# First quarter of the feed-forward input product as eight plain products instead of seven half-block products

## The chip, the core and the metric

The kernel runs on one core of one Trainium2 chip. The metric is device time in microseconds (us) of one execution; the median of several runs is compared. Engines: PE (TensorE, matrix products; PEld is its weight load), DVE (VectorE), ACT (ScalarE), POOL (GpSimd) and SP (SyncE, here a queue that issues transfers). Each engine takes its instructions in the order of its own queue and waits on semaphores for the others.

## The reference, cut to what matters

One block of an encoder: three token mixers, their gated sum through an output projection onto the residual x, then an RMS norm and a feed-forward part with squared ReLU. Sizes: 512 tokens, 1024 channels, 4096 hidden channels, all float32.

```python
        x = x + mixed @ w_out[l]

        u = _rmsnorm(x, g_mlp[l]) @ w_ff1[l]
        x = x + jnp.square(jax.nn.relu(u)) @ w_ff2[l]
```

## The kernel before

Every large product is made of three products in float32r: an operand is split into hi (rounded to float32r by ACT) and lo (what is left, by DVE), and hi*hi + hi*lo + lo*hi are added in PSUM. A weight tile is 128 x 1024 (512 KB); SP loads it as float32, ACT writes hi (`whi`), DVE writes lo (`wlo`), each into a ring of four buffers.

Since the norm's factor is one number per token, it is left out of u and put in behind: relu and square commute with it up to r squared, and `onto` (line 1137) multiplies by `r2` or `nr2` from `norm1` (line 1129).

The feed-forward part has four quarters of 1024 hidden channels (loop at line 1147). Each is `ff1` (line 1052: u times a quarter of w_ff1, then relu and square into `R`) and then ff2 (R times a quarter of w_ff2, added onto x). Both use Strassen's scheme in Winograd's form: a product of 2 x 2 blocks as seven half-block products instead of eight. For that sums of blocks of the weights are needed (loads that add onto what lies in the buffer, `w_more`, issued by POOL, line 186) and sums of blocks of the left operand. In ff1 a half-block product is 48 products of 256 columns (`product_f`, line 1032); in ff2 it is 24 products of 512 columns (`product`, line 162).

The left operand of ff1 is u, x transposed: `u_tile(f)` (line 936) makes four PE transposes of one block of 128 channels into one of two PSUM banks (tag `tr`) and ACT copies it out, times the gain of the norm, into `U`. `u_pair` splits a block of U, `u_form` a sum of blocks of U. The seven forms `us[0]` to `us[6]` are made once, during quarter one, and used by all four quarters. In `out_proj` (line 972), the last thing before, four u_tiles stand after the halves of the last product (line 1020), and the loads of the first quarter's weights are issued by `f_first` (line 965) into rings of tiles: `rq` (four buffers) and `raw` (three buffers).

Order: a scheduler puts the instructions of each engine in order when the kernel is built, near the order of the code but not bound to it, and gives a tile the buffer of one that is done; so a transfer waits on its queue until the buffer's last reader is done. SP's queue is strictly in order: a load that waits for its buffer holds up those behind it.

## Time and profile before

| what | value |
|---|---|
| median of 3 runs | 1144.14 us (1142.69 to 1144.30) |
| profiled execution | 1144.42 us |
| its span | 1142.6 us |
| PE busy | 1121.3 us (98%), 5784 instructions |
| DVE busy | 840.0 us (74%) |
| ACT busy | 701.4 us (61%) |
| mean granted clock of PE | 0.993 |

The profile is of one execution. The span runs from the first instruction to the last; the execution's time is 1.8 us longer. Busy time of PE counts overlapping products once, and each product's end is modelled, so a product's cost is read from the distance of starts in a stage without waits. "PEclk" or "granted clock" is the share of full speed that the chip grants PE: 1.0 is 2.4 GHz, and the lower level is 1.2 GHz; a value between is a mean over a stretch.

### The profile page before, as it was taken

What the parts mean: (1) busy time and instruction counts of PE and PEld (TensorE: products, weight loads), DVE (VectorE), ACT (ScalarE), POOL (GpSimd) and SP (SyncE); (2) the same over time, 40 slices, a digit from 0 to 9 for tenths busy, and PEclk for the clock granted to TensorE, in tenths of its full rate; (3) what the DMA queues carried; (4) which work ended last, traced back from release to release, by engine and by line L of the source; (5) the groups of instructions that cost most, each with busy time, mean ns of one, the idle gap of its engine ahead of it and who ended that gap; (6) DMA issues with size and microseconds to landing.
All of it is one profiled execution on the core that took longest, in us unless ns stands there. A gap on an engine that the chain in (4) does not pass through costs nothing.

```text
span 1142.6 us, 15585 instructions
## 1 busy us (share of the span) xinstructions
PE 1121.3 (98%) x5784; PEld 954.2 (84%) x5784; DVE 840.0 (74%) x1266; ACT 701.4 (61%) x1169; POOL 99.7 (9%) x159
## 2 busy tenths in 40 slices
PE   9899999999999999999999999999989999999998
PEld 6678888888888888878877888888888898998997
DVE  5998777764337877564488788679688779688788
ACT  7855468556426767754378788535667466475573
POOL 0012201000001000000000000001101111101110
PEclk9999999999999999999999999999989999999999
DMA  9969715114332221262222221748848978878774
GB/s 359 360 144 260 223 57 183 57 43 135 110 100 74 93 74 52 74 203 92 92 100 95 98 79 62 217 130 197 193 104 206 221 185 189 217 198 209 176 191 112
DMA packets 54275, 170.32 MB, mean 149 GB/s; under 512 B 5684, under 2 KB 12212, under 8 KB 54200
## 3 DMA queue, kind: packets, MB, share of 16 engines
q1 hardware_dynamic: 41192, 123.12, 30.8%
q0 software_dynamic: 12864, 46.14, 21.1%
q8 instruction: 45, 0.74, 0.3%
q14 instruction: 30, 0.25, 0.1%
q10 hardware_dynamic: 144, 0.07, 0.0%
HBM read 160.91 MB, written 8.40 MB: 148 GB/s over the span
## 4 chain that ended last, share of the span: by engine, by line
PE 53%; DVE 3%; ACT 3%; DMA 2%; issue 1%; DVEq 0%; ACTq 0%; POOLq 0%
PE pj L85 7%; PE pj L86 7%; PE pj L87 7%; PE q L171 3%; PE q L170 3%; PE q L172 3%; PE q L1044 3%; PE q L1045 3%; PE q L1043 3%; PE pj L171 1%; PE pj L170 1%; PE pj L172 1%; PE pj L1044 1%; PE pj L1043 1%; PE pj L1045 1%; DMA rq<-in_w_ff_dram 1%
## 5 line engine op out<-in xcount | busy, mean ns | idle before, releaser
L138 ACT ACTIVATE whi<-rq 128x1024 fp32r<-128x1024 f32 x126 | 132.3, 1056 | 116.3 <-DMA rq<-in_w_ff_dram 42.3
L85 PE MATMUL pj<-h,whi 128*128 128x512 f32 x512 | 202.0, 395 | 1.2 <-DVE u L778 0.7
L87 PE MATMUL pj<-h,wlo 128*128 128x512 f32 x512 | 200.3, 391 | 0.0
L86 PE MATMUL pj<-h,whi 128*128 128x512 f32 x512 | 200.2, 391 | 0.0
L139 DVE TENSOR_TENSOR wlo<-rq,whi 128x1024 fp32r<-128x1024 f32 x126 | 153.8, 1223 | 55.9 <-ACT whi L138 55.9
L81 DVE TENSOR_TENSOR wlo<-raw,whi 128x1024 fp32r<-128x1024 f32 x88 | 107.6, 1222 | 88.1 <-ACT whi L80 77.1
L80 ACT ACTIVATE whi<-raw 128x1024 fp32r<-128x1024 f32 x88 | 93.2, 1059 | 114.7 <-PE pj L86 114.7
L85 PEld LDWEIGHTS pj<-h,whi 128*128 128x128 f32 x512 | 96.5, 188 | 21.9 <-issue 1.1
L87 PEld LDWEIGHTS pj<-h,wlo 128*128 128x128 f32 x512 | 96.1, 188 | 20.0 <-issue 0.3
L86 PEld LDWEIGHTS pj<-h,whi 128*128 128x128 f32 x512 | 96.2, 188 | 19.0 <-issue 0.3
L171 PE MATMUL q<-wlo,shi 128*128 128x512 f32 (+1 forms) x236 | 91.1, 386 | 1.0 <-DVE wlo L139 1.0
L170 PE MATMUL q<-whi,shi 128*128 128x512 f32 (+1 forms) x236 | 91.1, 386 | 0.0
L172 PE MATMUL q<-whi,slo 128*128 128x512 f32 (+1 forms) x236 | 91.0, 385 | 0.0
L1043 PE MATMUL q<-u,whi 128*128 128x256 f32 x256 | 73.1, 286 | 3.7 <-ACT u L92 3.7
L85 PE MATMUL pj<-y,whi 128*128 128x512 f32 x192 | 74.9, 390 | 0.3 <-DVE gt L489 0.3
L86 PE MATMUL pj<-y,whi 128*128 128x512 f32 x192 | 74.7, 389 | 0.0
L87 PE MATMUL pj<-y,wlo 128*128 128x512 f32 x192 | 74.7, 389 | 0.0
L1044 PE MATMUL q<-u,whi 128*128 128x256 f32 x256 | 73.5, 287 | 0.0
L1045 PE MATMUL q<-u,wlo 128*128 128x256 f32 x256 | 73.4, 287 | 0.0
L189 POOL DMA_DIRECT2D rq<-in_w_ff_dram x56 | 48.3, 920 | 286.4 <-DVE wlo L139 159.0
L138 ACT ACTIVATE whi<-B 128x1024 fp32r<-128x1024 f32 x42 | 44.2, 1058 | 44.6 <-PE q L172 16.4
L139 DVE TENSOR_TENSOR wlo<-B,whi 128x1024 fp32r<-128x1024 f32 x42 | 51.0, 1225 | 19.0 <-ACT whi L138 19.0
(375 smaller groups left out, 2620.7 us busy)
## 6 DMA issues: line engine op xcount, KB each, us to landing
rq<-in_w_ff_dram SPq DMA_DIRECT2D x64, 512.0 KB, 5.0
rq<-in_w_ff_dram POOLq DMA_DIRECT2D x56, 512.0 KB, 5.7
B<-in_w_vo_dram SPq DMA_DIRECT2D x24, 512.0 KB, 5.8
raw<-in_w_gate_dram SPq DMA_DIRECT2D x24, 512.0 KB, 3.4
raw<-in_w_proj_dram SPq DMA_DIRECT2D x24, 512.0 KB, 3.4
raw<-in_w_sbqk_dram SPq DMA_DIRECT2D x16, 512.0 KB, 3.4
raw<-in_w_mlqk_dram SPq DMA_DIRECT2D x16, 512.0 KB, 3.4
rawk<-in_w_kv_dram SPq DMA_DIRECT2D x14, 512.0 KB, 8.4
```

What stands on the lines that cost most here:

```text
L81: dve.tensor_tensor(out=lo[:, c], in0=raw[:, c], in1=f32(hi[:, c]), op=ALU.subtract)
L85: pe.matmul(out, lh, rh, start=start, stop=False)
L86: pe.matmul(out, lh, rl, start=False, stop=False)
L87: pe.matmul(out, ll, rh, start=False, stop=stop)
L138: act.activation(out=hi, in_=raw, func=AF.Copy)
L139: dve.tensor_tensor(out=lo, in0=raw, in1=f32(hi), op=ALU.subtract)
L170: pe.matmul(banks[j][:, c], lh, w[0][:, cw], start=st, stop=False, **mm)
L171: pe.matmul(banks[j][:, c], lh, w[1][:, cw], start=False, stop=False, **mm)
L172: pe.matmul(banks[j][:, c], ll, w[0][:, cw], start=False, stop=sp_, **mm)
L1043: pe.matmul(o, wh, uh, start=start and k == 0 and f % 2 == 0, stop=False, **mm)
L1044: pe.matmul(o, wh, ul, start=False, stop=False, **mm)
L1045: pe.matmul(o, wl, uh, start=False, stop=stop and k == 3, **mm)
```

## The change

The first quarter's ff1 is no longer made of seven half-block products. A new function `ff1_0` makes its eight blocks of 128 hidden channels plainly, each as 8 blocks of k times three products of 512 columns (`ff1_plain`). Its weights lie in a new array `w_ff1a`, one contiguous 512 KB tile for each output, loaded and split by `load_w` (line 71, as in the gates and projections). `u_tile` now splits u itself out of PSUM (`split2`, ACT then DVE) into tiles `x1g`, all of u as hi and lo, and beside it still copies it as float32 into `U`. U now lies in the four buffers `rq`. The sums of u for the other three quarters are made from U by `u_forms`, called before outputs 2, 3 and 4 and after output 7; the sums are S3, S5, S6 and S4, the plain blocks are read from `x1g`. S4 takes the place of a block of `x1g` that is no longer read. The loads of ff2's first weights (`end(0)`) are called before output 6, both pairs into `rq`. The seven half-block products stay as they are for quarters two to four.

```diff
+    u = [None] * NK
     U = []
+    us = {}
 
     def u_tile(f):
 
-        if f % 4 == 0:
-            U.append(fpool.tile([P, 4, T], F32, tag="R", bufs=2, name="U"))
+        if f % 2 == 0:
+            U.append(fpool.tile([P, W], F32, tag="rq", bufs=4, name="U").rearrange("p (a b) -> p a b", a=2))
         r = tr()
         for i in range(NT):
             pe.transpose(r[:, i * P:(i + 1) * P], x1[i][f // 4][:, (f % 4) * P:(f % 4 + 1) * P], ident)
-        act.activation(out=U[f // 4][:, f % 4], in_=r, func=AF.Copy, scale=sm[:, C_GMLP + f:C_GMLP + f + 1])
-
-    def uA(kh, th):
-        return U[kh][:, :, 2 * th * P:2 * (th + 1) * P]
-
-    def u_pair(src):
-
-        n = len(us)
-        us.append([hp.tile([P, 4, 2 * P], F32R, tag="y", bufs=NK, name="u") if n < 4 else
-                   fpool.tile([P, 4, 2 * P], F32R, tag="u", bufs=6, name="u") for _ in range(2)])
-        split(*us[n], src)
-        return us[n]
-
-    us = []
+        u[f] = ytile("x1g")
+        g = sm[:, C_GMLP + f:C_GMLP + f + 1]
+        split2(u[f], r, g)
+        act.activation(out=U[f // 2][:, f % 2], in_=r, func=AF.Copy, scale=g)
+
+    def u_of(kh, th):
+        c = slice(2 * th * P, 2 * (th + 1) * P)
+        return lambda k: (u[4 * kh + k][:, 0, c], u[4 * kh + k][:, 1, c])
+
+    def u_sum(S, op, in0, in1):
+
+        for v in range(2):
+            def part(kh, th):
+                return U[2 * kh + v][:, :, 2 * th * P:2 * (th + 1) * P]
+            s_ = S(v) if callable(S) else S[:, 2 * v:2 * v + 2]
+            a = in0(v) if callable(in0) else part(*in0)
+            dve.tensor_tensor(out=s_, in0=a, in1=part(*in1), op=op)
+
+    def u_pair(name, S):
+        t = [fpool.tile([P, 4, 2 * P], F32R, tag="u", bufs=6, name="u") for _ in range(2)]
+        split(*t, S)
+        us[name] = lambda k: (t[0][:, k], t[1][:, k])
+
+    def u_forms(n):
+
+        if n == 0:
+            S = stile("Su")
+            u_sum(S, ALU.subtract, (0, 0), (0, 1))
+            u_pair("S3", S)
+        elif n == 1:
+            S = first["Su"] = stile("Su")
+            u_sum(S, ALU.subtract, (1, 1), (0, 1))
+            u_pair("S5", S)
+        elif n == 2:
+            S = first["Su"]
+            u_sum(S, ALU.add, lambda v: S[:, 2 * v:2 * v + 2], (0, 0))
+            u_pair("S6", S)
+            t = [hp.tile([P, 2, 2 * P], F32, tag="gate", bufs=NK, name="S4") for _ in range(2)]
+            u_sum(lambda v: t[v], ALU.subtract, lambda v: S[:, 2 * v:2 * v + 2], (1, 0))
+            first["S4"] = t
+        else:
+            for k in range(4):
+                hi, lo = u_of(0, 1)(k)
+                split(hi, lo, first["S4"][k // 2][:, k % 2])
+            us.update(A11=u_of(0, 0), A12=u_of(1, 0), A22=u_of(1, 1), S4=u_of(0, 1))
...
-        first["w11"] = w_pairs(first["F"][0])
-        u_pair(uA(0, 0))
-        u_form(ALU.subtract, uA(0, 0), uA(0, 1))
...
+    def ff1_plain(f, w, o, ks):
+        hi, lo = w
+        for k in ks:
+            mm3(o, hi[:, k * P:(k + 1) * P], lo[:, k * P:(k + 1) * P], u[k][:, 0, :], u[k][:, 1, :],
+                k == 0, k == NK - 1)
+
+    def ff1_0(R, end):
+
+        def out(f, o):
+            s = tmp("rs")
+            act.activation(out=s, in_=o, func=AF.Relu)
+            act.activation(out=R[f // 4][:, f % 4, :], in_=s, func=AF.Square)
+
+        ws, os = [], []
+        for f in range(2):
+            ws.append(load_w(w_ff1a[f]))
+            os.append(pj())
+            ff1_plain(f, ws[f], os[f], range(4))
+            u_tile(4 + 2 * f)
+            u_tile(5 + 2 * f)
+        norm1()
+        for f in range(2):
+            ff1_plain(f, ws[f], os[f], range(4, NK))
+            out(f, os[f])
+        for f in range(2, NK):
+            if f < 5:
+                u_forms(f - 2)
+            if f == 6:
+                end(0)
+            o = q4()
+            ff1_plain(f, load_w(w_ff1a[f]), o, range(NK))
+            out(f, o)
+        u_forms(3)
+        return end(1)
...
-        product_f(a, us[0], w11, True, False)
+        product_f(a, us["A11"], w11, True, False)
...
-        if qt == 0:
-            for f in range(4, NK):
-                u_tile(f)
-            S = stile("Su")
-            u_form(ALU.subtract, uA(1, 1), uA(0, 1), S)
...
-                B3 = w_raw2(w_ff2[qt], 1, 1)
+                B3 = (w_raw if qt == 0 else w_raw2)(w_ff2[qt], 1, 1)
...
-        w11, sp3 = ff1(qt, R, end)
+        w11, sp3 = ff1(qt, R, end) if qt else ff1_0(R, end)
...
+        "w_ff1a": cols(a["w_ff1"][0][:, :D])[0],
```

The order of PE behind the projection's last product, before. Names: `tr` are the two PSUM banks of transposes (the number tells one use from another), `x1_...` the rows of x that are transposed, `u_7335` and `u_7336` hi and lo of the first block of u, `pj` the bank of a product:

```order
L942 MATMUL tr_7321<-ident_76,x1_7114 128x128
L942 MATMUL tr_7498<-ident_76,x1_6786 128x128
L942 MATMUL tr_7498<-ident_76,x1_6788 128x128
L942 MATMUL tr_7498<-ident_76,x1_6782 128x128
L942 MATMUL tr_7498<-ident_76,x1_6784 128x128
L942 MATMUL tr_7504<-ident_76,x1_6786 128x128
L942 MATMUL tr_7504<-ident_76,x1_6788 128x128
L942 MATMUL tr_7504<-ident_76,x1_6782 128x128
L942 MATMUL tr_7504<-ident_76,x1_6784 128x128
L1043 MATMUL pj_7365<-u_7335,whi_7327 128x256
L1043 MATMUL pj_7366<-u_7335,whi_7327 128x256
L1044 MATMUL pj_7365<-u_7336,whi_7327 128x256
```

The first products stand behind all of these transposes: two of hi, then lo.

The same place on PE now. `x1g_7286` and `x1g_7295` are the first two blocks of u as split pairs, `whi_7351` and `whi_7389` the weights of outputs 0 and 1:

```order
L85 MATMUL pj_7356<-x1g_7286,whi_7351 128x512
L944 MATMUL tr_7312<-ident_76,x1_7108 128x128
L944 MATMUL tr_7312<-ident_76,x1_7110 128x128
L944 MATMUL tr_7312<-ident_76,x1_7112 128x128
L944 MATMUL tr_7312<-ident_76,x1_7114 128x128
L86 MATMUL pj_7356<-x1g_7286,whi_7351 128x512
L87 MATMUL pj_7356<-x1g_7286,wlo_7352 128x512
L85 MATMUL pj_7356<-x1g_7295,whi_7351 128x512
L86 MATMUL pj_7356<-x1g_7295,whi_7351 128x512
L87 MATMUL pj_7356<-x1g_7295,wlo_7352 128x512
L944 MATMUL tr_7321<-ident_76,x1_7108 128x128
L944 MATMUL tr_7321<-ident_76,x1_7110 128x128
```

A product of output 0 now stands right behind the projection, and the later transposes, four at a time, stand between products of outputs 0 and 1.

The order of ACT at that place, before. `sq` are the squares for the norm, `whi_7373` and `whi_7377` weights of the second product:

```order
L138 ACTIVATE whi_7373<-rq2_7224 128x1024
L943 ACTIVATE U_7290<-tr_7291,sm_70 128x512
L943 ACTIVATE U_7290<-tr_7297,sm_70 128x512
L932 ACTIVATE sq_7348,ssq_6635<-x1_6786 128x512
L138 ACTIVATE whi_7377<-rq2_7225 128x1024
L943 ACTIVATE U_7290<-tr_7315,sm_70 128x512
L943 ACTIVATE U_7290<-tr_7321,sm_70 128x512
L932 ACTIVATE sq_7351,ssq_6635<-x1_6788 128x512
L92 ACTIVATE u_7335<-U_7290 128x1024
L932 ACTIVATE sq_7354,ssq_6635<-x1_6782 128x512
L92 ACTIVATE u_7341<-Su_7339 128x1024
```

Each bank of transposes is read once, by the copy into U, and u is split from U.

The order of ACT there now (`whi_7476` and `whi_7517` are the weights of outputs 2 and 3):

```order
L80 ACTIVATE whi_7476<-raw_7475 128x1024
L95 ACTIVATE x1g_7286<-tr_7281,sm_70 128x512
L95 ACTIVATE x1g_7295<-tr_7290,sm_70 128x512
L948 ACTIVATE U_7280<-tr_7281,sm_70 128x512
L80 ACTIVATE whi_7517<-raw_7516 128x1024
L948 ACTIVATE U_7280<-tr_7290,sm_70 128x512
L95 ACTIVATE x1g_7317<-tr_7312,sm_70 128x512
L932 ACTIVATE sq_7333,ssq_6635<-x1_6786 128x512
L95 ACTIVATE x1g_7326<-tr_7321,sm_70 128x512
L948 ACTIVATE U_7311<-tr_7312,sm_70 128x512
L932 ACTIVATE sq_7336,ssq_6635<-x1_6788 128x512
```

Each bank is read twice by ACT, for hi and for U, and the second reading of the second bank stands behind a weight split.

The order of SP's loads from the last tile of the projection on, before:

```order
L889 DMA rq2_7105<-in_w_out_dram 128x1024
L889 DMA rq2_7224<-in_w_ff1_dram 128x1024
L882 DMA rq_7592<-in_w_ff1_dram 128x1024
L882 DMA rq_7593<-in_w_ff1_dram 128x1024
L889 DMA rq2_7225<-in_w_ff1_dram 128x1024
L889 DMA rq2_7431<-in_w_ff1_dram 128x1024
L889 DMA rq2_7432<-in_w_ff1_dram 128x1024
L889 DMA rq2_7813<-in_w_ff2_dram 128x1024
L889 DMA rq2_7814<-in_w_ff2_dram 128x1024
L889 DMA rq2_7991<-in_w_ff2_dram 128x1024
L882 DMA rq_7809<-in_w_ff2_dram 128x1024
```

The loads of the first quarter use both rings, `rq` and `raw` (`rq2` names tiles of the raw ring).

The same now:

```order
L79 DMA raw_7594<-in_w_ff1a_dram 128x1024
L79 DMA raw_7642<-in_w_ff1a_dram 128x1024
L79 DMA raw_7676<-in_w_ff1a_dram 128x1024
L889 DMA rq2_7817<-in_w_ff2_dram 128x1024
L882 DMA rq_7627<-in_w_ff2_dram 128x1024
L882 DMA rq_7628<-in_w_ff2_dram 128x1024
L882 DMA rq_7631<-in_w_ff2_dram 128x1024
L882 DMA rq_7632<-in_w_ff2_dram 128x1024
L889 DMA rq2_7818<-in_w_ff2_dram 128x1024
```

The plain weights go through the raw ring alone. The first weights of ff2 (`rq_7627`, `rq_7628` are B11, `rq_7631`, `rq_7632` B3) are queued behind them and behind a tile of B21, and take the four buffers that hold U.

## Rows read from the trace of the kernel before

**Rows 1.** The profile's page: span, and busy time of each engine.

```profile
span 1142.6 us, 15585 instructions
...
PE 1121.3 (98%) x5784; PEld 954.2 (84%) x5784; DVE 840.0 (74%) x1266; ACT 701.4 (61%) x1169; POOL 99.7 (9%) x159
```

**Rows 2.** Stretches of the span: bounds, length, busy us (instructions) by engine, clock, DMA.

```profile
810.38:865.19 54.81, 48.24 (x361) 46.86 (x360) 39.82 (x46) 37.60 (x55) 5.12 (x6) 0.91 0.61 145
814.00:819.00 5.00, 3.58 (x16) 3.38 (x17) 3.61 (x9) 4.22 (x10) 0.00 (x0) 0.66 0.81 251
834.00:840.00 6.00, 5.85 (x30) 5.73 (x29) 4.03 (x4) 1.70 (x3) 0.00 (x0) 0.54 0.00 0
903.28:943.60 40.32, 40.32 (x337) 40.31 (x336) 28.08 (x30) 25.09 (x32) 5.74 (x7) 1.00 0.79 196
```

**Rows 3.** Waits of PE, 770 to 945 us: total us, times, longest.

```profile
PE q L1043 <- ACT u L92: 3.7, 1, 3.7
PE tr L942 <- ACT U L943: 1.1, 1, 1.1
PE pj L1043 <- ACT u L92: 1.1, 2, 0.9
PE pj L1044 <- DVE u L93: 0.8, 1, 0.8
```

**Rows 4.** Timeline of PE at the hand-over: start, us, engine, line, operation, [idle before <-releaser].

```profile
806.77 1.03 PE L942 MATMUL tr<-ident,x 128*128 128x128 f32 x8
...
807.88 0.40 PE L171 MATMUL q<-wlo,shi 128*128 128x512 f32 x1
...
810.39 1.03 PE L942 MATMUL tr<-ident,x 128*128 128x128 f32 x8
812.52 1.24 PE L942 MATMUL tr<-ident,x 128*128 128x128 f32 x8 [1.10 <-ACT U L943]
```

**Rows 5.** Timeline of PE: where products of 512 and of 256 columns begin.

```profile
865.19 0.39 PE L170 MATMUL pj<-whi,shi 128*128 128x512 f32 x1
...
903.29 0.28 PE L1043 MATMUL pj<-u,whi 128*128 128x256 f32 x1
...
943.60 0.39 PE L170 MATMUL pj<-whi,shi 128*128 128x512 f32 x1
```

**Rows 6.** Timeline of ACT at the hand-over.

```profile
805.27 0.61 ACT L932 ACTIVATE sq<-x 128x512 f32<-128x512 f32 x1
...
807.02 1.06 ACT L138 ACTIVATE whi<-rq 128x1024 fp32r<-128x1024 f32 x1 [0.44 <-ACT sq L932]
807.98 1.25 ACT L943 ACTIVATE U<-tr,sm 128x512 f32<-128x512 f32 x2
```

**Rows 7.** Lines 95 and 96: count, duration ns min/median/max, first and last start.

```profile
L95 ACT ACTIVATE y<-tr,sm x8: 681/684/688, 629.5 to 729.6; 128x512 fp32r<-128x512 f32 x8
...
L96 DVE SCALAR_TENSOR_TENSOR y<-tr,sm,y x8: 741/751/753, 630.2 to 730.3; 128x512 fp32r<-128x512 f32 x8
```

**Rows 8.** Timeline of DVE, weight splits that free a load's buffer.

```profile
800.28 1.22 DVE L139 TENSOR_TENSOR wlo<-rq,whi 128x1024 fp32r<-128x1024 f32 x1
...
802.67 1.23 DVE L139 TENSOR_TENSOR wlo<-rq,whi 128x1024 fp32r<-128x1024 f32 x1
```

**Rows 9.** The page's part on transfers: count, size, median us to landing.

```profile
rq<-in_w_ff_dram SPq DMA_DIRECT2D x64, 512.0 KB, 5.0
rq<-in_w_ff_dram POOLq DMA_DIRECT2D x56, 512.0 KB, 5.7
...
raw<-in_w_gate_dram SPq DMA_DIRECT2D x24, 512.0 KB, 3.4
```

**Rows 10.** Timeline of PE after a wait of 2.09 us, 128x512 products.

```profile
623.61 0.47 PE L85 MATMUL q<-mqk 128*128 128x512 f32 x1 [2.09 <-DVE yt L862]
...
624.76 0.63 PE L86 MATMUL q<-mqk 128*128 128x512 f32 x1
625.18 0.63 PE L87 MATMUL q<-mqk 128*128 128x512 f32 x1
```

More of the change, by code (lines that the diff above doesn't have):

```diff
@@ L37, in tile_block @@
                w_sbqk, w_mlqk, w_vo, w_if, w_xq, w_gate, w_kv,
-               w_proj, w_out, w_ff1, w_ff2, out_):
+               w_proj, w_out, w_ff1a, w_ff1, w_ff2, out_):
     nc = tc.nc
@@ L956, in tile_block @@
-    us = []
-    first = {}
-    def u_form(op, in0, in1, S=None):
-        if S is None:
-            S = stile("Su")
-        dve.tensor_tensor(out=S, in0=in0, in1=in1, op=op)
-        return u_pair(S)
+        u[f] = ytile("x1g")
[5 more added lines that the diff above has]
+        return lambda k: (u[4 * kh + k][:, 0, c], u[4 * kh + k][:, 1, c])
@@ L965, in f_first @@
+    first = {}
     def f_first(qt):
-        F11 = w_raw(w_ff1[qt], 0, 0)
-        F3 = w_raw2(w_ff1[qt], 1, 1)
-        w_more(F3, w_ff1[qt], 1, 0)
+        F11 = w_raw(w_ff1[qt - 1], 0, 0)
+        F3 = w_raw2(w_ff1[qt - 1], 1, 1)
+        w_more(F3, w_ff1[qt - 1], 1, 0)
         first["F"] = F11, F3
@@ L1009, in out_proj @@
         w4 = w_pairs(B3)
-        f_first(0)
         for j in range(2):
@@ L1039, in product_f @@
                     wh, wl = ws[v][0][:, c], ws[v][1][:, c]
-                    uh, ul = up[0][:, k], up[1][:, k]
+                    uh, ul = up(k)
                     mm = dict(skip_group_check=True)
@@ L1057, in ff1 @@
         F11, F3 = first["F"]
-        G = w_ff1[qt]
+        G = w_ff1[qt - 1]
         a, c, d, e = [pj(), pj()], [q4(), q4()], [q4(), q4()], [tr(), tr()]
@@ L1081, in ff1 @@
             act.activation(out=X[j], in_=c[j], func=AF.Copy)
-        product_f(d, us[2], w5, True, False)
-        if qt == 0:
-            u_pair(uA(1, 0))
+        product_f(d, us["S5"], w5, True, False)
         F22 = w_raw(G, 1, 1)
@@ L1089, in ff1 @@
             dve.tensor_tensor(out=X[j], in0=X[j], in1=d[j], op=ALU.add)
-        product_f(a, us[3], w21, False, True)
-        if qt == 0:
-            u_form(ALU.add, S, uA(0, 0), S)
-            norm1()
+        product_f(a, us["A12"], w21, False, True)
         for v in range(2):
@@ L1099, in ff1 @@
             out(0, 0, j, a[j])
-        product_f(e, us[4], w6, True, True)
-        if qt == 0:
-            u_pair(uA(1, 1))
-            u_form(ALU.subtract, S, uA(1, 0), S)
+        product_f(e, us["S6"], w6, True, True)
         w22 = w_pairs(F22)
@@ L1109, in ff1 @@
             out(1, 1, j, X[j], -1.0)
-        product_f(c, us[5], w4, False, True)
+        product_f(c, us["A22"], w4, False, True)
         got = end(0)
@@ L1116, in ff1 @@
             out(1, 0, j, t)
-        product_f(d, us[6], w22, False, True)
+        product_f(d, us["S4"], w22, False, True)
         got += end(1)
@@ L1300 @@
         "w_out": wide(a["w_out"][0]),
-        "w_ff1": np.stack([wide(a["w_ff1"][0][:, i:i + D]) for i in range(0, 4 * D, D)]),
+        "w_ff1a": cols(a["w_ff1"][0][:, :D])[0],
+        "w_ff1": np.stack([wide(a["w_ff1"][0][:, i:i + D]) for i in range(D, 4 * D, D)]),
         "w_ff2": np.stack([wide(a["w_ff2"][0][i:i + D]) for i in range(0, 4 * D, D)]),
```

3 lines of the change are left out of this document (1 added, 2 removed).

## The prediction

> **What bounds the kernel now.** I read the page first: PE is busy 98% of a span of 1142.6 us, and no other engine above 84% [rows 1]. A share is an average, so next I cut the span into stretches, around the place that the change touches. The reader is to see two kinds of quarter in the feed-forward part. From 903.28 to 943.60 (the second quarter's seven products with w_ff1) PE is busy 40.32 of 40.32 us at a granted clock of 1.00. From 810.38 to 865.19, the same seven products of the first quarter with the transposes of u, it is busy only 48.24 of 54.81 us at a mean clock of 0.91 [rows 2]. So the first quarter alone is not bound by its products. The waits say what it is bound by: 3.7 us for one split of u, 1.1 for a copy of u out of PSUM, 1.1 and 0.8 for two more splits, 6.7 us in all [rows 3]. The timeline shows where: right behind the last product of the output projection PE does eight transposes, waits 1.10 us, does eight more, and waits for splits [rows 3, 4]. After both groups of waits the clock is at its lower level for a while, means of 0.66 and 0.54 [rows 2].
>
> **The terms.** A product of 512 columns costs, in a stage without waits, the 38.10 us from 865.19 to 903.29 over 168 products: 0.2268 us. One of 256 columns costs 40.31 us over 336: 0.1200 [rows 5].
>
> *Removed:* the seven half-block products of quarter one. The stage takes 54.80 us, from the transposes at 810.39 to the first product of ff2 at 865.19 [rows 4, 5]. Of it 336 x 0.1200 = 40.3 are products. Eight transposes cost 807.88 - 806.77 = 1.11 less the one product between, 0.88 us [rows 4]; the 24 that stand behind 810.39 cost 2.65. Waits are 6.7, and the rest, 5.1, is what the lower clock costs: a mean of 0.91 over 54.81 us means 9.9 us at half speed, so 4.9 lost if all of it was work [rows 2]. The parts meet.
>
> *Added:* eight plain products, 8 outputs x 8 blocks of k x 3 = 192 products of 512 columns, 192 x 0.2268 = 43.5 us. They are 3.2 us dearer than the seven in products alone. The same 24 transposes remain, 2.65. So without any wait the stage takes 46.2 us.
>
> The Trainium skill (TensorE: Matmul & The Clock Gate, section Back-to-back issue gap) gives N / 2.4 + 2.5 ns for a product, 215.8 and 109.2 ns here; the rows show 226.8 and 120.0, about 11 ns more each. By the page the plain products would be 4.7 us dearer instead of 3.2, and the forecast below 1138.4; the measured pace decides.
>
> *What is new as a wait.* Each block of u is now read three times from its PSUM bank: hi by ACT, lo by DVE, then the float32 copy by ACT; before, once. The bank is held for four transposes, 0.44, and 0.68 + 0.75 + about 0.68 us, some 2.6 [rows 4, 7]. There are two banks, so six blocks need at least 6 x 1.3 = 7.8 us. PE has between the start of the second half of the projection's last product and the last product of outputs 0 and 1 about 12 + 49 products and 24 transposes, 61 x 0.2268 + 2.65 = 16.5 us, with which the banks' turns are interleaved. ACT has in that time 16 passes over a bank at about 0.6 (two take 1.25), four squares at 0.61, three passes of 1024 columns at about 1.0 for two weights and one sum of u, and two small ones: 9.6 + 2.4 + 3.0 + 0.4 = 15.4 us [rows 6]. So ACT is just under PE, and PE will wait in short pieces only. Bounds: at the least six hand-overs of 0.05, 0.3 us; at the most each of four pairs of blocks waits as the first split did before, 4 x 0.9 = 3.6 [rows 3]. Walking the queues with the durations above I get nine tenths of a us in seven pieces, none over 0.2, and five returns from transposes to products at about 0.1; I take 1.4.
>
> *Weights.* The eight loads go into the ring of three. The first takes over a buffer of the projection as F3 did; the third and fourth follow the splits at 800.28 and 802.67, so they are issued at about 801.5 and 803.9 [rows 8]. Landing takes 3.4 us in the gates' stage, which has the same pattern, and 5.0 with the accumulating loads of ff around them [rows 9]. The third is needed when its hi buffer comes free at 807.02 [rows 6]: 0.5 to 2 us of slack. The projection's own end loses the loads of F11 and F3, so the short figure is nearer. Cost: nothing; if it is late by 1 us, ACT stands still with the first split of u behind it, and PE loses that 1 us.
>
> *The sums of u* (DVE and ACT) now hide beside outputs 2 to 6: they feed quarter two, not this one. In the old stage the 3.7 us stood exactly on them. The last sums of DVE fall at about 833 in my walk, since they stand behind the weight split of output 5. Only then do the four float32 copies leave the rq ring, and the weights of ff2 go in: the first lands at about 838 to 840, B3 is accumulated some 6 us later, about 851 [rows 9]. Product a needs B11 at 857, product c B3 at 862. Both are hidden, by 10 us or more.
>
> *The rest:* quarters two to four keep their instructions; their stages are full of products at clock 1.00 [rows 2], so nothing is won or lost there. The four late splits of S4 go beside output 7 and ff2's first product.
>
> Sum: 43.5 + 2.65 + 1.4 = 47.6 us in place of 54.8, 7.2 less. The profiled execution took 1144.42 us (1.8 around its span), so 1137.2; the median of the runs shown is 0.28 lower than it, so 1136.9 us. A difference under 0.2%, 2.3 us, cannot be told from none.
>
> **Rivals.**
> *The clock falls once.* A wait of 2.09 us elsewhere was followed by products of 512 columns 0.42 us apart (624.76 to 625.18), the lower level, 1.2 GHz, where full speed has 0.2268 [rows 5, 10]. In the old stage waits of 1.1, 0.9 and 0.8 between transposes had the same effect [rows 2, 3]. If the transposes in groups of four and short waits do it here too, the price is that of 3.4 us at half speed (the mean of 0.66 over 5 us [rows 2]): 8 products at 0.19 extra, 1.6; with waits at their upper bound, 3.6 in place of 1.4, the time is 1136.9 + 2.2 + 1.6 = 1140.7. For it: the fall stood at this very place, and ACT is nearly full. Against: the longest piece of my walk is 0.2 us.
>
> The Trainium skill (PSUM — Partial Sum Buffer, section PSUM bank collisions raise a hardware error) has it that two engines may not read one bank at once, reads against reads included, so the copy cannot run beside DVE's split; that is the ground of this rival, and no run here shows a collision.
>
> *The hand-over to ff2 becomes the stall.* ACT's queue has the squares of output 7, four splits of S4 and B3's second half in front of the split of S for the third product. If PE waits there as it did for the sum of u, 3.7 and then 2.8 at the lower clock (0.46 of 6 us) [rows 2, 3], 6.5 us go back: 1143.4, no change. Against: that product is due 10.9 us after output 7.
>
> *The weights of ff2 come late (slower).* The place is the rq ring: all four buffers hold u until DVE's last sum. If the sums slip to the end of the stage, 857, B11 lands at 862 and is split by 864.3, so PE waits 7.1; B3 lands, is accumulated (5.7 and two issues of 0.9) and split by 871, 1.2 after product c is due; then 2.8 at the lower clock: 11.1 in all, 1148.0 us. It decides from a last sum at about 848 on, and is slower than before from 853. Against: the sums stand in DVE's order between the splits for outputs 5 and 6, which PE's own progress paces.
>
> **How the numbers follow.** Forecast 0.70 (waits 0.3 to 3.6: 1135.8 to 1139.1); clock falls once 0.17; stall at ff2 0.08; weights late 0.05. Faster: 0.70 + 0.17 + 0.03 of the third, whose smaller stalls still leave 2.3 us, is 0.90; same 0.05; slower 0.05. The range takes in the forecast's own and the fallen clock, and below it 1 us, since the runs shown spread by 1.6: 1134.8 to 1141.0.
>
> **What would show it.** In the new profile the stage between the projection's last product and ff2's first should be 46.5 to 49.8 us long; its products 0.227 apart; the 3.7 us wait for a split of u gone; PE's waits there under 0.3 each; the clock 1.00 throughout; ff2's first weights landed by 845. Quarters two to four should keep their 78.4 us each (865.19 to 943.60) [rows 5]. I am wrong if a clock under 1.00 stands in that stage, if the first product of ff2 waits for a load or a split, or if a later quarter has grown.

## The result, and the profile after

| kernel | median of its runs | ratio to runs of before made beside it | 95% interval |
|---|---|---|---|
| before, beside it | 1144.22 us (4 runs, 1142.69 to 1145.48) | | |
| changed, first comparison | 1133.61 us (4 runs, 1133.37 to 1135.95) | 0.9908 | 0.9893 to 0.9922 |
| changed, timed again | 1135.76 us (6 runs, 1133.62 to 1138.56) | 0.9932 | 0.9917 to 0.9947 |

The change makes the kernel faster, and by more than was forecast: the first median lies 1.2 us below the range (1134.8 to 1141.0); the second lies inside it. All ten runs of the changed kernel together have a median of 1134.70 us, the 81 runs of the kernel before in all comparisons 1143.84; that is 9.1 us or 0.992, against a forecast of 7.2.

The page of the changed kernel, to be read against [rows 1]:

```profile
span 1131.7 us, 15270 instructions
...
PE 1117.8 (99%) x5640; PEld 943.5 (83%) x5640; DVE 826.8 (73%) x1260; ACT 694.8 (61%) x1167; POOL 94.7 (8%) x153
```

Its span is 10.9 us shorter than before's. The stretches that answer to [rows 2] (bounds, length, busy us and instructions of each engine, granted clock, DMA share, GB/s): the new stage of quarter one, two pieces of it, the first ff2, and the second quarter's seven products.

```profile
808.20:855.13 46.93, 46.92 (x217) 38.22 (x216) 29.71 (x43) 32.73 (x56) 4.28 (x5) 1.00 0.65 178
814.00:819.00 5.00, 5.00 (x29) 4.23 (x28) 4.18 (x7) 4.71 (x11) 0.00 (x0) 1.00 0.02 3
834.00:840.00 6.00, 6.00 (x28) 4.95 (x28) 4.85 (x5) 4.87 (x7) 1.71 (x2) 1.00 1.04 343
855.13:893.21 38.08, 38.08 (x169) 31.53 (x168) 32.48 (x33) 21.55 (x23) 6.02 (x7) 1.00 0.77 183
893.21:933.26 40.05, 40.05 (x337) 40.04 (x336) 27.28 (x29) 25.33 (x32) 5.17 (x6) 1.00 0.76 185
```

The stage takes 46.93 us where it took 54.80; PE is busy in all of it and the clock never leaves 1.00. The last row is the surprise: 40.05 us for the same 336 products that took 40.32. The timeline of PE (start, us, engine, line, operation, as in [rows 4, 5]) gives the bounds, from the first product behind the output projection to ff2's first, and the next quarter's start and end; the rows between them show the small gaps that are left:

```profile
808.20 0.39 PE L85 MATMUL pj<-x1g,whi 128*128 128x512 f32 x1
808.59 0.65 PE L944 MATMUL tr<-ident,x 128*128 128x128 f32 x4
809.00 0.48 PE L86 MATMUL pj<-x1g,whi 128*128 128x512 f32 x1
809.32 0.40 PE L87 MATMUL pj<-x1g,wlo 128*128 128x512 f32 x1
...
819.04 0.77 PE L85 MATMUL pj<-x1g,whi 128*128 128x512 f32 x2
819.65 0.39 PE L86 MATMUL pj<-x1g,whi 128*128 128x512 f32 x1
...
820.11 0.48 PE L86 MATMUL pj<-x1g,whi 128*128 128x512 f32 x1
820.43 0.40 PE L87 MATMUL pj<-x1g,wlo 128*128 128x512 f32 x1
...
855.13 0.39 PE L170 MATMUL pj<-whi,shi 128*128 128x512 f32 x1
...
893.21 0.28 PE L1067 MATMUL pj<-x1g,whi 128*128 128x256 f32 x1
...
933.26 0.40 PE L170 MATMUL pj<-whi,shi 128*128 128x512 f32 x1
```

The four waits of [rows 3] are gone: no wait of PE between 770 and 945 us is left. The largest of the whole span (total us, times, longest) lie elsewhere:

```profile
PE pj L86 <- DVE wlo L81: 2.9, 1, 2.9
PE q L85 <- DVE yt L862: 2.7, 3, 2.1
PE warm L232 <- DVE wz L202: 1.2, 1, 1.2
```

The difference of 10.9 us has three parts: 7.87 in the stage, 3 x 0.27 = 0.80 in quarters two to four, and 2.2 ahead of the change, in code that both kernels share. The clock's fall of [rows 10] behind the wait near 623 us, worth 1.5 us, is missing in this execution, and a wait at 67 us (the text of experiment 1 has 77) is 0.3 us long where it was 1.0. The experiments take the three parts one by one.

### The profile page after: what moved, and what is told of

Read it like the earlier page. It is cut to its first block, busy times and chain, and to the rows that moved or that the text cites. A ratio compares the mean times of both kernels' runs of the same rounds, so it can differ in the third digit from the quotient of the medians.

```text
span 1131.7 us, 15270 instructions
## 1 busy us (share of the span) xinstructions
PE 1117.8 (99%) x5640; PEld 943.5 (83%) x5640; DVE 826.8 (73%) x1260; ACT 694.8 (61%) x1167; POOL 94.7 (8%) x153
## 4 chain that ended last, share of the span: by engine, by line
PE 56%; DVE 3%; ACT 2%; issue 0%; DMA 0%; DVEq 0%; ACTq 0%; POOLq 0%
PE pj L85 7%; PE pj L87 7%; PE pj L86 7%; PE q L171 3%; PE q L170 3%; PE q L172 3%; PE q L1067 2%; PE q L1069 2%; PE q L1068 2%; PE q L85 2%; PE q L86 2%; PE q L87 2%; PE pj L170 2%; PE pj L171 2%; PE pj L172 2%; PE pj L1068 1%
## 5 line engine op out<-in xcount | busy, mean ns | idle before, releaser
L138 ACT ACTIVATE whi<-rq 128x1024 fp32r<-128x1024 f32 x112 | 117.5, 1056 | 110.5 <-DMA rq<-in_w_ff_dram 40.5
L81 DVE TENSOR_TENSOR wlo<-raw,whi 128x1024 fp32r<-128x1024 f32 x96 | 117.3, 1221 | 92.8 <-ACT whi L80 81.7
L139 DVE TENSOR_TENSOR wlo<-rq,whi 128x1024 fp32r<-128x1024 f32 x112 | 136.4, 1220 | 59.0 <-ACT whi L138 57.1
L80 ACT ACTIVATE whi<-raw 128x1024 fp32r<-128x1024 f32 x96 | 101.6, 1059 | 121.7 <-PE pj L86 115.1
L189 POOL DMA_DIRECT2D rq<-in_w_ff_dram x50 | 43.1, 909 | 284.2 <-DVE wlo L139 179.7
L171 PEld LDWEIGHTS q<-wlo,shi 128*128 128x128 f32 x236 | 44.3, 188 | 9.6 <-DVE wlo L139 0.7
L170 PEld LDWEIGHTS q<-whi,shi 128*128 128x128 f32 x236 | 44.3, 188 | 8.9
L172 PEld LDWEIGHTS q<-whi,slo 128*128 128x128 f32 x236 | 44.3, 188 | 8.8
```

What stands on the lines that cost most here:

```text
L80: act.activation(out=hi[:, c], in_=raw[:, c], func=AF.Copy)
L81: dve.tensor_tensor(out=lo[:, c], in0=raw[:, c], in1=f32(hi[:, c]), op=ALU.subtract)
L138: act.activation(out=hi, in_=raw, func=AF.Copy)
L139: dve.tensor_tensor(out=lo, in0=raw, in1=f32(hi), op=ALU.subtract)
L170: pe.matmul(banks[j][:, c], lh, w[0][:, cw], start=st, stop=False, **mm)
L171: pe.matmul(banks[j][:, c], lh, w[1][:, cw], start=False, stop=False, **mm)
```

## Experiments

Stage means the time from the end of the output projection's last product to ff2's first product. A ratio is always to runs of the kernel before made beside the kernel that is named. The changed kernel itself ran only in the two comparisons above, so the other kernels are set against it through these ratios.

**1. Is the part ahead of the change chance?** Both kernels again, unedited.

> The kernel before, unchanged, profiled and timed once more. In its first profile the clock fell for 1.5 us near 624 us (granted clock 0.57 from 624 to 628) after a wait of TensorE of 2.1 us, and a wait near 77 us was 0.7 us longer than in the profile of the changed kernel; both lie in code that the change leaves alone, and together they are 2.2 of the 10.9 us between the two profiled executions. Theory (chance): this execution shows one or both of them in another size, its span comes out anywhere between about 1140.5 and 1144, the mean clock of the single executions spreads from 0.993 to 0.998, and the fast ones reach about 1142.5. Rival (belongs to the program): the fall at 624 us stands there again with the same 1.5 us, span 1142.6 within 0.3, and every execution of this kernel has it.

> The changed kernel, unchanged, profiled and timed once more. By the terms that can be put down to the change (stage of quarter one 7.87 us shorter, quarters two to four 0.27 us each) the true difference is 8.7 us, so that if the 2.2 us ahead of the change are chance, executions without a fall differ by 8.7 us: about 1133.5 against 1142.3, and some executions of the changed kernel show the fall too, about 1.5 to 2 us longer (1135.5). Rival: the 2.2 us belong to the two programs, and the difference stays 10.6 (ratio 0.9907) with no fall ever in the changed kernel.

Before: 1143.82 us (11 runs), ratio 1.0001 (0.9992 to 1.0011). Of the first theory, the wait at 67 us came in another size (0.4 us) and the fastest run is near the figure named (1141.89). But the fall stands there again, the span is 1144.3 us, and the mean clock of the eleven executions lies between 0.991 and 0.994. The stretch behind the wait:

```profile
622.83:626.83 4.00, 4.00 (x15) 3.68 (x16) 4.00 (x8) 3.97 (x7) 0.00 (x0) 0.65 0.35 95
```

Changed: 1135.76 us, 7.8 below the runs beside it where the first comparison had 10.6. Now the changed kernel shows the fall as well. Its timeline and the stretch behind the wait:

```profile
624.50 0.67 PE L85 MATMUL q<-mqk 128*128 128x512 f32 x1 [2.12 <-DVE yt L862]
624.97 0.63 PE L86 MATMUL q<-mqk 128*128 128x512 f32 x1
625.39 0.63 PE L87 MATMUL q<-mqk 128*128 128x512 f32 x1
```

```profile
624.50:628.50 4.00, 4.00 (x12) 3.44 (x13) 4.00 (x8) 3.96 (x7) 0.00 (x0) 0.57 0.30 90
```

In the first profile of the same kernel the same wait was followed by a clock of 1.00:

```profile
623.00:627.00 4.00, 4.00 (x25) 3.75 (x26) 4.00 (x8) 3.97 (x7) 0.00 (x0) 1.00 0.32 100
```

The old stage varies as well: in the second profile of the kernel before it took 56.4 us in place of 54.80, mostly since a wait of 1.1 us [rows 3] was 2.4:

```profile
809.57:865.96 56.39, 48.48 (x362) 47.10 (x361) 39.81 (x46) 37.61 (x55) 5.14 (x6) 0.91 0.61 146
...
PE tr L942 <- ACT U L943: 2.4, 1, 2.4
```

Over all kernels here that have the wait near 623 us, 10 of 15 profiled executions show the fall and 5 do not. The wait is the same (2.08 to 2.12 us). The changed kernel shows both outcomes, so for one and the same program it is chance. Of the kernels built on the one before, 5 of 6 fall, of those built on the changed one 5 of 9; whether the kernel before falls more often is not settled by so few. The Trainium skill (TensorE: Matmul & The Clock Gate, section What's actually happening) says of a kernel's start that the same kernel runs a varying number of products at the lower clock. The rows show such a variation in mid-kernel too.

**2. Does the place of the moving tile set its pace?** In the built programs one thing differs in quarters two to four, the place of six tiles `u`, the halves of three forms. They begin 32 bytes past a multiple of 256 in the kernel before (products five to seven) and 160 in the changed one (products two, three and five). All other operands of these products, x1g and the weights too, begin at 192.

```diff
     def u_pair(name, S):
+        fpool.tile([P, 32], F32, tag="pad", name="pad")
         t = [fpool.tile(...      # the line goes on as before
```

> The changed kernel with 128 bytes of unused space ahead of the tiles u (the halves of S3, S5 and S6), so that they begin at the same place within 256 bytes as in the kernel before. Nothing else moves. Theory (the pace of a 256-column product depends on where its moving tile begins): products two, three and five of quarters two to four go back from 5.68 to about 5.76 us of 48 pairs of instructions, a quarter's stage from 40.05 to about 40.31 us, the whole 0.7 to 0.8 us longer than the changed kernel. Rival (the pace comes from other things: which forms are held in u, one tile for both halves in x1g, what other engines write then): 40.05 us stay, and the time is that of the changed kernel within 0.3 us.

> The kernel before with 128 bytes of unused space ahead of those of its tiles u that lie in the last pool (the halves of S6, A22 and S4, products five to seven), so that they begin where u begins in the changed kernel. Theory (place of the moving tile): these three products fall from 5.76 to about 5.68 us in each quarter, a quarter's stage from 40.31 to about 40.07 us, and the whole is about 0.9 us shorter in four quarters (ratio 0.9992). Rival: 40.31 us stay and the time is that of the kernel before.

(The second has the same line ahead of the tiles `u` of the last pool.) The second quarter's stage, first of the changed kernel with u moved back, then of the kernel before with u moved:

```profile
895.06:935.36 40.30, 40.30 (x337) 40.29 (x336) 28.75 (x31) 24.86 (x32) 6.02 (x7) 1.00 0.83 198
```

```profile
902.75:942.82 40.07, 40.07 (x337) 40.07 (x336) 28.54 (x31) 24.97 (x32) 6.00 (x7) 1.00 0.82 198
```

Both go where the theory puts them, in every quarter; product by product, 5.76 and 5.68 us change places. The whole times, 1135.62 (ratio 0.9924, 0.9912 to 0.9936) and 1143.04 (0.9989, 0.9978 to 1.0000), cannot resolve 0.8 us by themselves. The part of 0.8 us is a side effect of the order in which tiles are allocated.

**3. Which places are good?** Three runs that move more tiles.

```diff
 the probe, in u_pair:
+        n = {"S3": 16, "S5": 32, "S6": 40}[name]
+        fpool.tile([P, n], F32, tag="pad" + name, name="pad")
 activations and u at 160, behind the line that makes the pool hp:
+    hp.tile([P, 56], F32, tag="pad", name="pad")
 instead of it, weights too at 160, behind the line that makes the pool wp:
+    wp.tile([P, 56], F32, tag="pad", name="pad")
 and in both, in u_pair:
+        fpool.tile([P, 8], F32, tag="padu", name="padu")
```

> The changed kernel with unused space ahead of each form of u, so that S3 begins 224 bytes, S5 96 bytes and S6 0 bytes past a multiple of 256 (in the changed kernel 160 for all three; x1g 192, where a product takes 5.76 us). Theory (the place of the moving tile within some power of two of bytes sets the pace of 48 pairs): each of products two, three and five takes one of the two values 5.68 and 5.76 us, the same in all three quarters, and the three offsets tell which places are fast. Rival (only places that are no multiple of 64, seen at 32 as a change of the steps' pattern, differ): 0 is at 5.76 us and 224 and 96 show a pattern of their own. No gain of the whole above 0.3 us is expected.

> The changed kernel with 224 bytes of unused space ahead of the tiles of activations (and 32 ahead of u), so that the moving operand of the projections and of all of ff1 begins 160 bytes past a multiple of 256, while the weights stay at 192; in ff2 and the output projection, where the weights move, the moving operand stays at 192 and the loaded one is at 160. Theory (place of the moving tile alone): the four products on x1g go to 5.68 us too, 0.29 us a quarter; 512-column products of the projections and of quarter one save the same 1.6 ns each, some 2400 of them 3.9 us; in all about 4 to 5 us below the changed kernel's runs. Rival (only 256-column products are paced so, or the place of both operands to each other counts): 0.9 us at most.

> As the one before, with the unused 224 bytes ahead of the tiles of weights, so that weights, activations and u all begin 160 bytes past a multiple of 256. Theory (place of the moving tile alone): ff2 and the output projection are faster too, about 1.6 ns for each of some 5000 products, 7 to 8 us below the changed kernel's runs, and a quarter's ff1 stage is 39.8 us. Rival (what counts is that moving and loaded operand begin at different places): products on x1g and u go back to 5.76 us, a quarter's stage is 40.3 us and the whole is as long as the changed kernel or 0.7 us longer.

The probe (one run, 1133.91 us) gave 5.66, 5.69 and 5.66 us for S3, S5 and S6, values of their own, so neither theory of two levels holds. The other two decide between place and distance. Activations moved alone (the second quarter's stage, then a group of the page: busy us, mean ns of one):

```profile
910.65:950.42 39.77, 39.77 (x338) 39.77 (x337) 27.08 (x29) 25.21 (x32) 5.16 (x6) 1.00 0.77 186
```

```profile
L87 PE MATMUL pj<-h,whi 128*128 128x512 f32 x512 | 203.1, 397 | 0.0
```

Activations and weights moved together:

```profile
895.63:935.94 40.31, 40.31 (x337) 40.31 (x336) 27.40 (x29) 25.30 (x32) 5.18 (x6) 1.00 0.79 187
```

```profile
L87 PE MATMUL pj<-h,whi 128*128 128x512 f32 x512 | 200.2, 391 | 0.0
```

With the two operands apart, products of 256 columns are faster (5.68 us each time) and those of 512 slower (397 against 391 ns; starts 0.2333 apart in place of 0.2268), and the whole takes 1153.51 us, ratio 1.0084 (1.0065 to 1.0103): my 4 to 5 us of gain became a loss of 19 against the changed kernel. With both moved, every pace is the old one, 1136.62 us (0.9929, 0.9906 to 0.9951). So the distance between the moving and the loaded operand counts, not the place of either. Not every distance changes the pace: the tiles `u` of the kernel before lie 160 bytes below the weights, and their products take the same 5.76 us. The Trainium skill (TensorE: Matmul & The Clock Gate, section Step-by-step: what each phase is for) says that loading the next weights takes no read bandwidth from the running product. These runs show that the pace still depends on where the two operands lie to each other; whether it is the reads that meet was not tried.

```diff
-        u[f] = ytile("x1g")
+        u[f] = ytile("x1g", 8 * f)      # tile f begins 32 f bytes later
```

> The changed kernel with each of the eight tiles x1g shifted: tile k begins 32 k bytes further from its slot's start than tile 0, whose start lies at the same 192 of 256 as the weights (slots are 256 bytes longer for it). So product k of every output of quarter one, and of the forms A11, A12, A22 and S4 in the other quarters, shows the pace at a distance of 0, 32, 64, up to 224 bytes between the moving operand and the loaded one. Theory (the distance of the two operands within 256 bytes sets the pace, as the runs with one or both tiles shifted suggest): 0 gives 0.2268 us for 512 columns and 224 (one step below) gives 0.233, as they did there; 256 columns give 0.120 and 0.118; the others take values of their own, and one of them may be below 0.2268 for 512 columns, which would be worth up to 5000 products times the difference. Rival (distance does not matter for 512 columns beyond zero or not zero): all seven shifted places show 0.233.

One run: 1133.28 us. With distances mixed, all eight groups of 512-column products are slower, 0.2311 to 0.2343 us apart in the mean where the changed kernel has 0.2267 for each; the group at 0 bytes too (0.2313). So a product's own distance is not all that sets its pace; that its neighbours' distances count as well is a reading that no run separates. Six outputs took 33.25 us in place of 32.41. The 256-column stages fell to 39.73 us from 40.05. The rival was nearer: for 512 columns equal places are the best of those tried, and as x1g serves both widths, what the later quarters win (3 x 0.32 us) quarter one loses.

**4. Was the stage lost to waits on u?** Quarter one's products read a tile that is ready.

```diff
+        up = us
+        if qt == 0:
+            r4 = [t_.rearrange("p a b -> p a b") for t_ in first["sp4"]]
+            up = [r4] * 7
-        product_f(a, us[0], w11, True, False)
+        product_f(a, up[0], w11, True, False)
 ... and so for all seven
```

> The kernel before, in which the seven products of quarter one read as their moving operand the halves of the last mixed tile (ready before the stage begins) in place of those of u; all tiles of u are still made and quarters two to four read them. The first quarter of the output's inner sum is therefore another. Theory (the stage of 54.8 us loses its time by waits on u alone, and by the clock that falls after them): the stage falls to its products and transposes, 40.3 + 2.65 = 43.0, at most 44 us with one wait at the transposes, the granted clock stays at 1.00, and the whole is 10.8 to 11.8 us shorter than the kernel before, 3 us shorter than the changed kernel: the plain products win the waits and give 3.2 us of them back in product time. Rival (weights of the seven products or free banks are as late as u): the stage stays above 48 us, with waits on the halves of the weights or on evictions in place of those on u.

The stage and the first ff2; then PE's only wait there, and ACT just ahead of it:

```profile
807.27:850.45 43.18, 43.16 (x361) 42.95 (x360) 36.99 (x44) 32.31 (x49) 3.83 (x5) 1.00 0.66 170
...
850.45:893.45 43.00, 40.79 (x170) 32.38 (x169) 36.22 (x37) 26.84 (x32) 7.58 (x10) 0.96 0.83 197
```

```profile
PE q L170 <- ACT shi L92: 2.1, 1, 2.1
...
856.10 1.04 ACT L138 ACTIVATE whi<-rq 128x1024 fp32r<-128x1024 f32 x1
857.04 1.04 ACT L92 ACTIVATE shi<-S 128x1024 fp32r<-128x1024 f32 x1
```

The stage falls by 11.6 us to its products and transposes, as the theory has it. But 4.9 us of that come back in ff2 (43.00 against 38.08): its second product now waits for the split of S3, which ACT, without a pause there, reaches only at 857.04, and the clock falls behind that wait. The whole is 1136.82 us, ratio 0.9938 (0.9918 to 0.9958), less gain than the 10.8 to 11.8 expected. This is a stall of the kind that the prediction's rival "hand-over to ff2" describes, at ff2's second product and behind weight splits, where the rival has the third and the splits of S4. Of the kernels here it is the only one with a wait at that place, and its stage is the shortest.

**5. Direct split or plain products?** The change also splits u straight from the transposes in PSUM. Each half alone:

```diff
 before, with the direct split of A11 (the tiles us[0] are made at f == 0):
+        if f < 4:
+            split(us[0][0][:, f], us[0][1][:, f], r[:, :2 * P], g)
         act.activation(out=U[f // 4][:, f % 4], in_=r, func=AF.Copy, scale=g)
 ...
-        u_pair(uA(0, 0))
 changed kernel, without it:
-        split2(u[f], r, g)
         act.activation(out=U[f // 2][:, f % 2], in_=r, func=AF.Copy, scale=g)
+        split2(u[f], U[f // 2][:, f % 2])
```

> The kernel before with one idea of the change alone: the first form of u (A11) is split straight from the transposes in PSUM, not from the copies in U; the seven half-block products of quarter one and all else stay. Theory (the stage loses its time because forms made one after another, S3 above all, are not ready when their product is due, and the plain products are what covers this): the first product starts about 1 us sooner, the wait for S3 (3.7 us in the kernel before) grows by about as much, because its copies stand behind the splits, the stage falls by 0 to 1.5 us of 54.8, and the whole is within 1.5 us of the kernel before. Rival (the long chain copy, split, product is the loss, and the direct split what saves it): the stage falls below 50 us and the whole by 5 us or more.

> The changed kernel with the direct split undone: each tile x1g is split from its copy in U (the copy first, then the halves), all else stays. Theory A (the direct split is most of the gain wherever it stands): the stage of quarter one grows by 3 us or more over 46.9, with waits on the halves of x1g, and the clock falls behind them. Theory B (plain products do not need it: a block of them has 4 x 0.68 us of work for the engines to run ahead): the first products wait 0.5 to 1 us longer, one copy and its release, the stage is 47.4 to 48 us, the whole 0.5 to 1 us longer.

The stage of the kernel before with the direct split, and PE's waits there; then the stage of the changed kernel without it:

```profile
813.81:863.24 49.43, 45.26 (x362) 44.39 (x362) 39.49 (x48) 37.69 (x57) 5.17 (x6) 0.97 0.68 163
```

```profile
PE q L1047 <- ACT u L92: 3.7, 1, 3.7
PE pj L1047 <- ACT u L92: 0.4, 1, 0.4
```

```profile
812.92:859.60 46.68, 46.66 (x218) 38.42 (x216) 29.04 (x43) 31.45 (x54) 4.27 (x5) 1.00 0.65 180
```

My theory fell in the first, and the rival's figures came true: the direct split alone takes 5.4 us off the stage (54.80 to 49.43), 1138.32 us or 0.9954 (0.9938 to 0.9970), since the early waits of 1.1, 0.9 and 0.8 us and the clock's first fall go. The wait of 3.7 us, which I had put on S3, is the third product's, for S5, and stays. In the second, theory A fell, and B held but for its price: plain products need no direct split at all (46.68 us; 1135.82 us in 4 runs, 0.9929, 0.9913 to 0.9946). Either cure removes the early waits. Of the two only the plain products also remove the last one; the reading is that blocks 4 to 7 are then needed one by one and no sum is. Their order also brings the transposes forward: the last eight begin at 820.45, 7.5 us into the stage, where the kernel before has them at 828.64, 18 us into it. Experiment 6 adds that alone to the direct split.

**6. Can seven products do without the last wait, and better?**

```diff
+        if qt == 0:
+            for f in range(4, NK):
+                u_tile(f)                 # the last 16 transposes, one product sooner
         product_f(c, us[1], w3, True, False)
 and, in the second kernel, also the pad ahead of u, and ahead of the wait near 623 us:
+        if head == 1:
+            fill = tr()
+            for _ in range(9):
+                pe.matmul(fill, k[0][0][:, 0, :P], q[0][0][:, 0, :], start=True, stop=True)
```

> The seven half-block products in quarter one with the direct split, and the last sixteen transposes issued before the product of S3 instead of behind it (one product, 5.76 us, sooner). Theory (the wait of 3.7 us is the chain transposes, copy, difference, split, and nothing else): the wait for S5 goes, the stage from the last eight transposes to ff2 is 44 to 45 us against 46.9 of the changed kernel and 49.5 of the direct split alone, and the whole comes to 1133 to 1135 us, as long as the changed kernel or up to 2 us shorter. Rival (ScalarE, busy all of 814 to 824 us in the run with the direct split, is the bound by then): a wait of 1 to 3 us stays or moves to ff2's second product, which waited 2.1 us when the seven products did not wait for u, and the whole is 1135 to 1137 us.

> The one before, with the two other edits that runs pointed to: u of products five to seven begins where it is paced faster (four quarters of 0.24 us), and nine unread products fill TensorE's wait near 623 us, where the clock fell in most executions. The theories add up: 1.0 us for the place, 1.2 to 1.8 for the filled wait, together 2 to 3 us less than the one before, 1130.5 to 1133 us, the fastest of all kernels here. Rival (the gains overlap, or ff2's wait takes the place): not below 1132.9 us, where the changed kernel with the filled wait stands.

Stage and first ff2 of the first kernel, and PE's waits in these two stretches:

```profile
808.99:853.98 44.99, 43.90 (x361) 43.12 (x361) 39.05 (x48) 37.41 (x57) 5.15 (x6) 1.00 0.72 176
853.98:893.19 39.21, 38.45 (x170) 31.45 (x169) 32.66 (x34) 22.71 (x26) 5.93 (x7) 1.00 0.81 198
```

```profile
PE q L171 <- DVE wlo L139: 0.8, 1, 0.8
PE q L1048 <- DVE u L93: 0.8, 1, 0.8
PE q L1047 <- ACT u L92: 0.2, 1, 0.2
```

The wait of 3.7 falls to 0.2 + 0.8, and the stage, 44.99 us as the theory has it, is 1.9 us shorter than the changed kernel's. The first ff2 gives 1.1 back, with a wait of 0.8 for the split of a weight near its end (at 890.5 us), not at ff2's second product; the slower pace of quarters two to four gives 0.8 back. So 1135.96 us, 0.9930 (0.9915 to 0.9945), the rival's figure: no difference from the changed kernel that these runs resolve. With all edits 1134.48 (5 runs), 0.9917 (0.9903 to 0.9931), not the sum that was expected; its profiled execution has the shortest span of all profiled ones, 1130.3 us, but its runs cannot be told from the changed kernel's.

**7. Are the sums hidden, and does filling the wait hold the clock?** The first kernel leaves the four sums of u out (S3, S5, S6 and S4 read blocks of x1g); the second is the changed kernel with the nine products shown above.

```diff
-                u_forms(f - 2)
...
-        u_forms(3)
+        us.update(A11=u_of(0, 0), ..., S3=u_of(0, 0), S5=u_of(1, 1), S6=u_of(0, 0))
```

> The changed kernel without the sums of u: S3, S5, S6 and S4 are not made, quarters two to four read blocks of x1g in their place (so three quarters of the inner sums are other values). Theory (the sums are hidden beside quarter one's outputs): the stage of quarter one stays 46.9 us within 0.1. Products two, three and five then move x1g, which begins at the same place as the weights, so each goes from 5.68 to 5.76 us, and the whole is 0.6 to 0.8 us longer, not shorter. Rival (the sums delay evictions or ff2's first halves): the stage or ff2 of quarter one is shorter by 0.5 us or more.

> The changed kernel with nine products of 512 columns, whose result nobody reads, put into TensorE's wait of 2.1 us near 623 us (for the bank that the last yt frees; nine at 0.2268 us are 2.04 us). Theory (the fall of the clock behind this wait, seen in some executions and not in others, makes the spread and the 1.5 us of the first comparison): the granted clock stays at 1.00 near 625 us, no execution shows the fall, and the median is 1133.5 to 1134.3, 0.5 to 1.5 us below the changed kernel's runs (1134.7 over ten), with a smaller spread. Rival (the fall does not come from the wait, or the spread from other things): the fall is still seen, or the median stays at 1134.7 and the spread at 5 us.

Without sums, the stage:

```profile
808.77:855.68 46.91, 46.91 (x217) 38.29 (x216) 20.17 (x28) 29.25 (x49) 4.28 (x5) 1.00 0.68 179
```

0.02 us shorter with 9.5 us less work on DVE: the sums are hidden. The stages of quarters two to four go to 40.31 us, as expected. Whole: 1134.74 us, 0.9921 (0.9895 to 0.9947). With the wait filled, the timeline there and the stretch behind it:

```profile
620.40 2.20 PE L809 MATMUL tr<-mqk 128*128 128x512 f32 x9
622.66 0.47 PE L85 MATMUL q<-mqk 128*128 128x512 f32 x1
```

```profile
622.66:626.66 4.00, 4.00 (x25) 3.74 (x26) 4.00 (x8) 3.96 (x7) 0.00 (x0) 1.00 0.31 90
```

The clock stays at 1.00, there and in the other kernel with the fill. The median is 1132.91 us (6 runs), 0.9908 (0.9886 to 0.9930), the lowest of all kernels here. Yet one run of six took 1136.2, so other chance remains, and the interval overlaps the changed kernel's: likely better by about a us, not shown.

## Why the prediction was right and where it was wrong

The forecast was 1136.9 us, the profiled execution of the changed kernel took 1133.5. The 3.4 us between them are 0.7 of waits that did not come, 0.8 won in quarters that were put at nothing, and 1.9 of the base. The mechanism was right for the stage that the change touches. One step was wrong, that the later quarters win nothing; one term, the waits, was twice too large; the rest is the base.

- *The stage is lost to waits on u and the clock behind them*: right. With the waits taken away it falls to 43.2 us at a clock of 1.00, where products and transposes alone were put at 43.0 (experiment 4).
- *Products and transposes, 43.5 + 2.65 = 46.2*: right; the plain products start 0.2267 us apart where no transposes stand between them.
- *Waits 1.4*: mis-sized. The term was 0.9 for seven short waits and 0.5 for five returns from transposes to products. What stands beyond 46.2 is 0.7 us (46.93), none of it a wait that the trace lists. The returns are real (809.00 to 809.32 is 0.32 us, 0.09 more than the pace), but 2.65, which is three times the 0.88 measured up to the second product behind the transposes, held three of the five already. Gaps between products and transposes make up some 0.4 (808.20 to 808.59, the two products from 819.04, 820.11 to 820.43). 0.7 us of the miss.
- *Weights and sums hidden*: right. No wait for a load; the stage is the same without the sums; the last sum on DVE ends at 830.4 us (my walk: 833) and ff2's first weight is split from 838.8.
- *Quarters two to four: nothing is won or lost there*: this step failed. They win 0.27 us each, 0.80 in all, because the change's other allocation order moved u to another distance from the weights (experiment 2). I had not looked at where tiles lie, and had read the pace of 0.1200 us as belonging to the width alone. The formula of the Trainium skill that stands beside it in the prediction (TensorE: Matmul & The Clock Gate, section Back-to-back issue gap) is given there for one isolated product, not for a stream of them; the sum does not rest on it.
- *The base of 1144.42 us*: that execution carried a fall of the clock and a longer early wait, 2.2 us that the first profile of the changed kernel has not; 0.28 of it the forecast had taken off already. By their mean clocks (0.997 to 0.998) the four runs of the first comparison were mostly without such a fall, the six of the second were mixed (0.995 to 0.998), and their median lies in the range: this part of the miss is luck. Against the 81 runs the forecast saving of 7.2 plus 0.7 and 0.8 is 8.7, and 1143.84 - 8.7 = 1135.1; the ten runs have 1134.7. The range reached only 1 us below the forecast's own, for a spread of the runs that was 1.6 us in the three shown and is 5.2 in the ten of the changed kernel.
- *Rivals*: the clock fell nowhere in the stage. The stall at the hand-over to ff2 did not occur; one like it does in experiment 4. The weights of ff2 were not late.
- What the prediction did not ask: whether plain products were the only way. The direct split alone brings over half of the gain, and seven products with direct split and earlier transposes as much as the plain ones, within what the runs resolve. The plain products do without the direct split; they have the earlier transposes by their order. Seven products with earlier transposes and no direct split were not run.

## What to carry to other kernels

When a scheme with fewer products needs sums or forms that are not ready, first ask what the products' order waits for: here, cutting the chain at its head and issuing the transposes one product sooner brought as much as the dearer products that need no sums. A saving that makes a stage shorter than its successor's preparation can come back as a wait there (4.9 of 11.6 us in experiment 4). And before a stage is called unchanged, compare the addresses of its operands in both programs, and several profiles of the same kernel: here 0.8 us were allocation and up to 2.2 chance.

## What the runs showed of the hardware

- The pace of products with a weight load each depends on the distance between the two operands' addresses. With the places taken modulo 256 bytes, 256 columns take 0.1200 us when moving and loaded operand begin at equal places and when the moving one lies 160 bytes below, 0.1183 at 32 below and 0.1179 at 32 above; 512 columns take 0.2268 at equal places and 0.2333 at 32 bytes apart either way (experiments 2 and 3). Why it is so was not tried.
- The same wait of 2.1 us on PE is followed by a stretch at the lower clock level, worth some 1.5 us, in 10 of 15 profiled executions and by none in 5. With nine unread products in the wait, the clock stayed at 1.00 in both of two.
